# Gates that leave PSUM unscaled: the multiplication by 1/rms moves from the evacuation to the place of use

## The chip, the cores and the metric

The kernel runs on one core of a Trainium2 chip. The metric is the device time of one execution in microseconds (us). Five engines work side by side, each through a queue of its own in program order: TensorE (PE in the profile; its weight loads are listed apart as PEld), VectorE (DVE), ScalarE (ACT), GpSimd (POOL) and SyncE (SP, which here only issues DMAs). They are ordered among each other by semaphores. Matmul results land in PSUM and are copied from there ("evacuated") by VectorE or ScalarE into SBUF.

## The reference

One layer of an encoder on x of 1024 tokens by 1024 features, float32:

```
h    = rms_norm(x, norm_g)
proj = h @ w_in                 # 1536 Hyena columns, 512 gate g_h, q, k, v, 512 gate g_a
y_h  = order-2 Hyena of the 1536 columns (short convolution, then two long FFT convolutions)
y_a  = windowed attention of q, k, v (+-128 tokens, 8 query heads, 2 key heads, a sink)
y    = concat(rms_norm(y_h) * silu(g_h), rms_norm(y_a) * silu(g_a))
x    = x + y @ w_out
```

The first rms_norm has two factors: the weight norm_g per feature, which the kernel puts into its operands, and 1/rms per token. Since a token's 1/rms is the same for all features, it can be applied after the projection: the kernel projects x * norm_g and multiplies the columns of proj, one per token, by the token's 1/rms. The change is about where that is done for g_h and g_a.

## The kernel before, in words

The projection works on tiles of 128 output columns in two halves of 512 tokens, so that a half is a PSUM tile of 128 x 512 with tokens along the free side. Its 8 steps over the features take three matmuls each (L257 to L259: both operands are split into a high and a low part, `w_hi`/`w_lo` and `h`), 24 matmuls for a half. There are two PSUM banks for these halves (`pj`), used in turn. `self.row` holds 1/rms of the 1024 tokens in all 128 partitions.

The order of the projection tiles is a string: Hyena and q/k/v tiles first, then eight gate tiles: four of the Hyena branch (c = 0 to 3), four of attention (c = 4 to 7). `gate_tiles` (L441) computes them; its `evac` calls `scaled` (L268), a VectorE product of the PSUM tile and `self.row` at a raised priority, into one of three SBUF buffers tagged `raw` (named `graw`), and SyncE stores that in the DRAM scratch `gt`. The Hyena tiles use `scaled` too, and are not touched.

Beside the projections runs the other branch, the generator `hyena_branch`: filter spectra, DFTs and inverse DFTs of four quarters of 128 channels, then attention. `weave` mixes the two by fixed costs per step, and a scheduler with priorities then fixes the order of instructions on each engine. The last Hyena quarter ends with VectorE's products `u` (L803) and ScalarE's squares `zsq` (L834), whose sum over quarters is `ztot`. After it attention starts: for every block of 128 tokens q is transposed (aT, bT), scores are computed twice, once for the maxima (`smax`, reduced by VectorE at L945 into `mx`) and once transposed (`st`), VectorE adds a mask to the edges (L983), ScalarE takes the exponential `pf` (L986), TensorE multiplies by the values (`pv`) and VectorE divides (`den`, `ao`).

The gates come back at two places:

- `hyena_output(c)` runs four times between the attention units, behind the sum `ztot` on each engine queue that it uses together with it. It reloads a whole gate row of 128 x 1024 (two buffers, tag `sc`), takes silu as x * (1 + tanh(x/2)) (L1063 on ScalarE, L1064 on VectorE, the factor 1/2 being elsewhere), multiplies with the transposed Hyena output and splits the product into `yh` and `yl`.
- `output_operands(j)` runs once per block of 128 tokens. It reloads 128 x 4 x 128 of the attention gates (tag `ga`, two buffers, so that the load for block j waits until the last reader of block j - 2, the subtraction `al` at L1109, is done), takes silu the same way, multiplies with the transposed attention output and splits it into `ah` and `al`.

The output projection (`po`, L1124 to L1126) takes these operands and the split w_out. The first half of w_out is staged in eight pieces (`output_weights`, while the last gate tiles are projected): POOL issues the load (L1031), ScalarE casts the high part (L1037), VectorE subtracts the low part (L1038); two buffers. The first `po` matmul stands behind the last gate projection. `last_weights` stages the second half in the same way from buffers of the stage pool.

Of the kernel before, what the change touches and what calls it, by code (L numbers as in the profile page):

```python
# [14 lines left out]
ALU = mybir.AluOpType  # L15
# [4 lines left out]
P = 128  # L20
# [21 lines left out]
HP = 200  # L42
# [8 lines left out]
def view(ap, off, dims):  # L51
    return bass.AP(
        tensor=ap.tensor, offset=ap.offset + off, ap=[list(ap.ap[0])] + [list(d) for d in dims]
    )


class Kernel:
# [387 lines left out]
    def gate_tiles(self, cs, sp):  # L445

        nc = self.nc
        ws = [self.next_weights(c) for c in cs]
        pieces = None
        for h in range(2):  # L450
            for c, w in zip(cs, ws):
                if len(cs) > 1 and h == 1 and c == cs[1]:
                    assert self.mixed
                    last = self.last_weights(sp)
                    next(last)

                def evac(h, pt):
                    raw = sp.tile([P, 512], F32, tag="raw", name=self.nm("graw"))
                    self.scaled(raw, pt, h)
                    nc.sync.dma_start(self.gt[:, c, 512 * h : 512 * h + 512], raw)  # L460

                for cost in self.half(w, h, evac):
                    yield cost
                    if pieces:
                        next(pieces, None)
            if len(cs) > 1 and h == 0:
                pieces = self.output_weights()
                next(pieces)
        if len(cs) > 1:
            for _ in chain(pieces, last):  # L470
                pass
        self.gates += len(cs)
# [593 lines left out]
    def hyena_output(self, c, rstd, sp, ps):  # L1066

        nc = self.nc
        V = nc.vector
        g = sp.tile([P, S], F32, tag="sc", name=self.nm("gate"))  # L1070
        nc.sync.dma_start(g, self.gt[:, c])
        self.silu2(g, sp, "t2")
        y = sp.tile([P, 8, P], F32, tag="raw", name=self.nm("y"))
        nc.sync.dma_start(y, self.zd[c])
        V.tensor_tensor(out=y, in0=y, in1=view(rstd, 0, [[1, 8], [0, P]]), op=ALU.mult)
        for h in range(2):
            pt = ps.tile([P, 4, P], F32, tag="t", name=self.nm("yT"))
            for k in range(4):
                nc.tensor.transpose(pt[:, k], y[:, 4 * h + k], self.ident)
            gv = g.rearrange("p (b a) -> p a b", a=8)[:, 4 * h : 4 * h + 4]  # L1080
            V.scalar_tensor_tensor(
                out=gv, in0=pt, scalar=self.gn[:, c : c + 1], in1=gv, op0=ALU.mult, op1=ALU.mult
            )
        nc.scalar.copy(self.yh[:, c], g)
        V.tensor_tensor(out=self.yl[:, c], in0=g, in1=self.yh[:, c].bitcast(F32), op=ALU.subtract)
# [6 lines left out]
    def output_operands(self, j, op, ps):  # L1092

        nc = self.nc
        V = nc.vector
        rows = slice(j * P, (j + 1) * P)
        g = op.tile([P, 4, P], F32, tag="ga", name=self.nm("ga"))
        nc.sync.dma_start(g, self.gt[:, 4:8, rows])
        self.silu2(g, op, "th")
        of = op.tile([P, 512], F32, tag="of", name=self.nm("of"))  # L1100
        nc.sync.dma_start(of, self.od[j])
        pt = ps.tile([P, 4, P], F32, tag="t", name=self.nm("oT"))
        for c in range(4):
            nc.tensor.transpose(pt[:, c], of[:, c * P : (c + 1) * P], self.ident)
        V.tensor_tensor(out=g, in0=pt, in1=g, op=ALU.mult)
        ah = op.tile([P, 4, P], F32R, tag="ah", name=self.nm("ah"), bufs=3)
        al = op.tile([P, 4, P], F32R, tag="al", name=self.nm("al"), bufs=3)
        nc.scalar.copy(ah, g)
        V.tensor_tensor(out=al, in0=g, in1=ah.bitcast(F32), op=ALU.subtract)  # L1109
        return ah, al  # L1110
# [383 lines left out]
```

## Time and profile before

| | us |
|---|---|
| runs | 641.06, 640.04, 639.3 |
| median | 640.04 |
| the profiled execution's own time | 637.56 |
| its span, first to last instruction | 635.8 |
| PE busy / DVE busy / ACT busy in the span | 625.0 / 531.2 / 266.5 |

The profiled execution is a run of its own, a little faster than the three timed ones. Between its span and its time lie 1.76 us at the start and the end. PE's busy time counts a matmul from its start to its modelled end, and matmuls overlap in a pipeline, so it hides short stalls. The granted clock of TensorE is 1.0 throughout. In the timeline `us` is how long an instruction took, and what stands in brackets is how long its engine was idle before it and what released it.

The sixteen gate halves are evacuated between 340.5 and 473.4 us, the first `ztot` is at 408.2, the gates of the Hyena branch are used until 445 (tanh product), those of attention from 491 to 598.

### The profile page before, as it was taken

The numbers are of one execution on the slowest core, as the hardware profiler recorded it, in microseconds if no ns is written. First come the engines' busy times: TensorE is split into PE (matmuls) and PEld (weight loads), VectorE is DVE, ScalarE is ACT, GpSimd is POOL, SyncE is SP. The second block draws the span as 40 slices with busy tenths as digits, with TensorE's granted clock in tenths as the row PEclk, the third lists the DMA queues.
The fourth block names the chain that finished last, engine by engine and source line by source line (L and its number), as shares of the span: only waits on it lengthen the run. The fifth ranks groups of instructions, "written<-read, shape, count | busy, mean of one in ns | idle before, by whom it ended". The sixth has DMA issues, their size and how long they took to land.

```text
span 635.8 us, 10699 instructions
## 1 busy us (share of the span) xinstructions
PE 625.0 (98%) x3994; PEld 553.1 (87%) x3994; DVE 531.2 (84%) x1189; ACT 266.5 (42%) x506; POOL 65.3 (10%) x83
## 2 busy tenths in 40 slices
PE   9999999999999999999999999999998999999997
PEld 7878998989898989899998988888787878888885
DVE  6969699997999997979999899689989888976531
ACT  6766413254432353523443332545465343544210
POOL 0121002021100121211102102100200000000000
PEclk9999999999999999999999999999999999999999
DMA  8966937478574576694548656645645125313321
GB/s 324 281 148 155 296 86 181 126 180 202 147 182 129 148 184 160 138 216 107 134 135 208 184 175 156 188 138 182 207 137 179 56 65 166 105 37 114 100 82 51
DMA packets 47107, 98.37 MB, mean 155 GB/s; under 512 B 6728, under 2 KB 15440, under 8 KB 46800
## 3 DMA queue, kind: packets, MB, share of 16 engines
q1 hardware_dynamic: 32784, 63.79, 30.2%
q0 software_dynamic: 10720, 26.21, 21.8%
q10 hardware_dynamic: 3552, 7.71, 3.5%
q8 instruction: 31, 0.51, 0.3%
q14 instruction: 20, 0.16, 0.1%
HBM read 53.65 MB, written 22.02 MB: 119 GB/s over the span
## 4 chain that ended last, share of the span: by engine, by line
PE 85%; DMA 5%; DVE 4%; issue 3%; ACT 2%; POOL 0%; SPq 0%; POOLq 0%; ACTq 0%; DVEq 0%
PE proj L257 10%; PE proj L258 9%; PE proj L259 9%; PE dft L645 8%; PE pv L1000 5%; PE fw L761 5%; PE po L1124 4%; PE po L1126 4%; PE po L1125 4%; PE inv L802 4%; PE qkv L508 3%; PE qkv L509 3%; PE qkv L510 3%; PE smax L940 1%; PE uT L434 1%
## 5 line engine op out<-in xcount | busy, mean ns | idle before, releaser
L257 PE MATMUL proj<-h,w_hi 128*128 128x512 f32 x304 | 121.5, 400 | 0.0
L259 PE MATMUL proj<-h,w_lo 128*128 128x512 f32 x304 | 119.8, 395 | 0.0
L258 PE MATMUL proj<-h,w_hi 128*128 128x512 f32 x304 | 119.7, 394 | 0.0
L225 POOL DMA_DIRECT2D w_lo<-wraw x48 | 42.2, 896 | 242.3 <-ACT w_lo L224 220.3
L258 PEld LDWEIGHTS proj<-h,w_hi 128*128 128x128 f32 x304 | 57.2, 188 | 11.4 <-issue 0.7
L257 PEld LDWEIGHTS proj<-h,w_hi 128*128 128x128 f32 x304 | 57.2, 188 | 11.3 <-issue 0.7
L259 PEld LDWEIGHTS proj<-h,w_lo 128*128 128x128 f32 x304 | 57.1, 188 | 10.9
L508 PE MATMUL qkv<-w_hi,h 128*128 128x256 f32 x192 | 55.0, 287 | 0.0
L510 PE MATMUL qkv<-w_hi,h 128*128 128x256 f32 x192 | 54.6, 285 | 0.0
L509 PE MATMUL qkv<-w_lo,h 128*128 128x256 f32 x192 | 54.4, 284 | 0.0
L222 ACT CAST w_hi<-wraw 128x512 fp32r<-128x512 f32 x48 | 29.4, 619 | 59.7 <-PE proj L258 36.6
L645 PE MATMUL dft<-eo,d 128*128 128x128 f32 x352 | 45.5, 276 | 1.5 <-DVE eo L629 1.5
L1000 PEld LDWEIGHTS pv<-vv,pf 128*128 128x128 f32 x352 | 44.6, 191 | 2.0 <-DVE ao L1005 0.4
L1000 PE MATMUL pv<-vv,pf 128*128 128x66 f32 x352 | 45.0, 269 | 0.1
L645 PEld LDWEIGHTS dft<-eo,d 128*128 128x128 f32 x352 | 42.5, 192 | 2.0 <-DVE eo L629 1.9
L508 PEld LDWEIGHTS qkv<-w_hi,h 128*128 128x128 f32 x192 | 36.7, 191 | 0.0
L509 PEld LDWEIGHTS qkv<-w_lo,h 128*128 128x128 f32 x192 | 36.7, 191 | 0.0
L510 PEld LDWEIGHTS qkv<-w_hi,h 128*128 128x128 f32 x192 | 36.7, 191 | 0.0
L945 DVE CUSTOM_DVE_ANT_0 mj<-smax,mask 128x384 f32<-128x384 f32 (+1 forms) x64 | 33.2, 519 | 3.7 <-PE smax L940 2.2
L986 ACT ACTIVATE pf<-st 128x768 f32<-128x768 f32 (+1 forms) x32 | 24.3, 758 | 25.5 <-DVE st L983 24.9
L802 PE MATMUL inv<-V,di 128*128 128x128 f32 x256 | 34.8, 275 | 0.0
L1128 DVE TENSOR_TENSOR xr<-po,xr 128x512 f32<-128x512 f32 x22 | 15.1, 688 | 22.0 <-PE po L1126 22.0
(217 smaller groups left out, 1458.2 us busy)
## 6 DMA issues: line engine op xcount, KB each, us to landing
wraw<-in_w_in SPq DMA_DIRECT2D x48, 256.0 KB, 3.7
w_lo<-wraw POOLq DMA_DIRECT2D x48, 256.0 KB, 4.2
hy<-hsc ACTq DMA_DIRECT2D x12, 512.0 KB, 5.9
u<-hy SPq DMA_DIRECT2D x12, 512.0 KB, 6.1
hsc<-hs POOLq DMA_DIRECT2D x9, 511.5 KB, 5.3
hsc<-hraw POOLq DMA_DIRECT2D x9, 511.5 KB, 5.4
x<-in_x_t SPq DMA_DIRECT2D x8, 512.0 KB, 8.9
dec<-in_decay SPq DMA_DIRECT2D x8, 512.0 KB, 4.2
```

Source lines behind the costliest of these rows:

```text
L225: nc.gpsimd.dma_start(l.bitcast(F32), raw, accum_op=ALU.add)
L257: nc.tensor.matmul(pt, hi[:, k], xh, start=k == 0, stop=False)
L258: nc.tensor.matmul(pt, hi[:, k], xl, start=False, stop=False)
L259: i = nc.tensor.matmul(pt, lo[:, k], xh, start=False, stop=k == 7)
L508: nc.tensor.matmul(pt[:, b], hh, hi[:, :, k], start=k == 0, stop=False)
L509: nc.tensor.matmul(pt[:, b], hh, lo[:, :, k], start=False, stop=False)
L510: i = nc.tensor.matmul(pt[:, b], hl, hi[:, :, k], start=False, stop=k == 7)
L645: nc.tensor.matmul(out, m, eo[:, t, e], start=n == 0, stop=n == len(terms) - 1)
L761: nc.tensor.matmul(pt[:, k, c], self.d[:, t + k, c], u[:, t + k], start=True, stop=True)
L802: nc.tensor.matmul(pt[:, k], self.di[:, t + k, c], v[:, t + k, c], start=c == 0, stop=c == 1)
L945: V.tensor_tensor_reduce(out=junk[:, 0:nk], in0=pm[:, 0:nk], in1=mask, op0=ALU.add, op1=ALU.max, scale=1.0, scalar=NEG, accum_out=mx[:, 4 ...
L1000: nc.tensor.matmul(pv[:, h], probs[:, n, cols], self.vv[:, k0 + n, g], start=n == 0, stop=n == nk - 1)
```

## The change

ScalarE copies the gate halves out of PSUM as they are, at the same raised priority, and they are stored so. VectorE multiplies the reloaded gates by `self.row`, in place, before silu: 4 times 128 x 1024 in `hyena_output`, 8 times 128 x 512 in `output_operands`, where the 128 tokens of the block are read four times over.

```diff
@@ gate_tiles, evac @@
                     raw = sp.tile([P, 512], F32, tag="raw", name=self.nm("graw"))
-                    self.scaled(raw, pt, h)
+                    with self.tc.high_priority(HP):
+                        nc.scalar.copy(raw, pt)
                     nc.sync.dma_start(self.gt[:, c, 512 * h : 512 * h + 512], raw)
@@ hyena_output @@
         g = sp.tile([P, S], F32, tag="sc", name=self.nm("gate"))
         nc.sync.dma_start(g, self.gt[:, c])
+        V.tensor_tensor(out=g, in0=g, in1=self.row.rearrange("p h t -> p (h t)"), op=ALU.mult)
         self.silu2(g, sp, "t2")
@@ output_operands @@
         g = op.tile([P, 4, P], F32, tag="ga", name=self.nm("ga"))
         nc.sync.dma_start(g, self.gt[:, 4:8, rows])
+        V.tensor_tensor(out=g, in0=g, in1=view(self.row[:], j * P, [[0, 4], [1, P]]), op=ALU.mult)
         self.silu2(g, op, "th")
```

Lines move by one behind the first edit and by more behind the second and third (the tanh of L1063 is L1064 in the changed kernel, the silu product of L1064 is L1065; the new products are L1073 and L1101). Up to the last Hyena quarter the engines' orders differ only by the moved evacuations. At three places more moves.

On VectorE at the end of the last Hyena quarter, before (`inv` is the inverse transform in PSUM, `kk` belongs to attention's keys, `mx` to the first block's maxima):

```order
L270 TENSOR_TENSOR graw_4083<-proj_3973,row 128x512
L748 SCALAR_TENSOR_TENSOR V_3809<-gm_3821,ml_3811 128x2x128
L803 TENSOR_TENSOR u_3774<-inv_3856,u_3774 128x512
L803 TENSOR_TENSOR u_3774<-inv_3866,u_3774 128x512
L910 TENSOR_TENSOR kk_3986<-qkv_3980,kk_3986 128x2x64
L910 TENSOR_TENSOR kk_4107<-qkv_4101,kk_4107 128x2x64
L1288 TENSOR_REDUCE ztot<-zssq 128x8
L1064 SCALAR_TENSOR_TENSOR gate_4344<-th_4346,gate_4344 128x1024
L270 TENSOR_TENSOR graw_4220<-proj_4086,row 128x512
L945 ISA mj_4022,mx_4005<-smax_4020,mask_3929 128x256
```

and after the change:

```order
L804 TENSOR_TENSOR u_3774<-inv_3856,u_3774 128x512
L804 TENSOR_TENSOR u_3774<-inv_3866,u_3774 128x512
L1291 TENSOR_REDUCE ztot<-zssq 128x8
L1073 TENSOR_TENSOR gate_4344<-gate_4344,row 128x1024
L95 TENSOR_SCALAR rsv_4328<-ztot 128x8
L96 TENSOR_SCALAR rsh_4329<-ztot 128x8
L1073 TENSOR_TENSOR gate_4386<-gate_4386,row 128x1024
L911 TENSOR_TENSOR kk_3986<-qkv_3980,kk_3986 128x2x64
L99 TENSOR_SCALAR rsy_4331<-rsv_4328 128x8
L108 TENSOR_TENSOR rst_4330<-rsy_4331 128x8
L1065 SCALAR_TENSOR_TENSOR gate_4344<-th_4347,gate_4344 128x1024
```

The evacuations of `graw` are gone; two products of 128 x 1024 stand between `ztot` and the first tanh product, and the keys' subtraction comes after them.

On TensorE at attention's first transposes (`aT`), before:

```order
L258 MATMUL proj_4086<-h_90,w_hi 128x512
L259 MATMUL proj_4086<-h_90,w_lo 128x512
L257 MATMUL proj_4243<-h_89,w_hi 128x512
L933 MATMUL aT_4006<-identr,qq_3946 128x128 x4
L933 MATMUL aT_4013<-identr,qq_3946 128x128 x4
L258 MATMUL proj_4243<-h_89,w_hi 128x512
```

and after the change:

```order
L259 MATMUL proj_4086<-h_90,w_lo 128x512
L934 MATMUL aT_4006<-identr,qq_3946 128x128 x4
L257 MATMUL proj_4086<-h_90,w_hi 128x512
L258 MATMUL proj_4086<-h_90,w_hi 128x512
L934 MATMUL aT_4013<-identr,qq_3946 128x128 x4
L941 MATMUL smax_4020<-kt_3940,qa_4011 128x256
```

The transposes stand ten projection matmuls earlier, inside the gate half `proj_4086`.

On VectorE in one of the later attention blocks, after the change (`al_6082` is the last reader of the buffer into which `ga_6400` is loaded):

```order
L1112 TENSOR_TENSOR al_6082<-ga_6067,ah_6081 128x512
L984 TENSOR_TENSOR st_6184<-st_6184,mask_3929 128x256
L1004 TENSOR_TENSOR den_6211<-pv_6204,es_5897 128x2
L1005 RECIPROCAL den_6211<-den_6211 128x2
L1006 TENSOR_TENSOR ao_5998<-pv_6204,den_6211 128x128
L984 TENSOR_TENSOR st_6215<-st_6215,mask_3929 128x256
L1101 TENSOR_TENSOR ga_6400<-ga_6400,row 128x512
L95 TENSOR_SCALAR rsv_6299<-ossq_6297 128x1
```

Before, the first VectorE instruction of this gate was its tanh product at the same place; now the product with `row` stands there, and the tanh product five small instructions later.

## Prediction

> **What bounds the kernel now.** I read the busy table and the chain of waits of the page first, then a table of windows, because the gates live only in the last half of the span.
>
> ```profile
> PE 625.0 (98%) x3994; PEld 553.1 (87%) x3994; DVE 531.2 (84%) x1189; ACT 266.5 (42%) x506; POOL 65.3 (10%) x83
> ...
> PE 85%; DMA 5%; DVE 4%; issue 3%; ACT 2%; POOL 0%; SPq 0%; POOLq 0%; ACTq 0%; DVEq 0%
> ...
> 340.00:400.00 60.00, 60.00 (x341) 52.42 (x340) 55.62 (x93) 18.48 (x37) 7.79 (x9) 1.00 0.66 178
> 400.00:420.00 20.00, 19.88 (x122) 16.19 (x121) 11.81 (x44) 11.28 (x39) 2.86 (x4) 1.00 0.64 188
> 420.00:460.00 40.00, 39.50 (x254) 34.12 (x253) 38.45 (x84) 19.70 (x35) 3.78 (x7) 1.00 0.54 175
> 460.00:480.00 20.00, 19.27 (x125) 16.83 (x125) 16.62 (x59) 12.36 (x21) 1.61 (x3) 1.00 0.47 158
> 480.00:545.00 65.00, 62.53 (x387) 52.11 (x386) 55.97 (x193) 27.51 (x56) 0.00 (x0) 1.00 0.33 104
> 545.00:580.00 35.00, 35.00 (x241) 30.52 (x239) 28.14 (x107) 16.20 (x33) 0.00 (x0) 1.00 0.27 91
> 580.00:606.00 26.00, 25.84 (x157) 22.52 (x157) 13.80 (x54) 9.04 (x18) 0.00 (x0) 1.00 0.25 83
> ```
>
> The columns of a window are its length, then the busy time of PE, PEld, DVE, ACT and POOL with counts, then the granted clock, the DMA share and GB/s. TensorE sets the end: 98% of the span and 85% of the chain, at a full clock. It isn't held up at all between 340 and 400, where the first nine gate halves are evacuated. It loses time from 420 on, most of all in 480 to 545 (2.5 of 65 us), the stretch where VectorE is 56.0/65 = 86% busy. Whom it waits for there is in the waits of TensorE's weight loads from 400 to the end (total, times, longest):
>
> ```profile
> PEld st L977 <- ACT pf L986: 3.4, 7, 1.2
> PEld smax L940 <- DVE mx L945: 2.9, 7, 0.9
> PEld st L978 <- ACT qb L963: 1.9, 5, 0.5
> PEld smax L940 <- ACT qa L935: 1.5, 5, 0.7
> ```
>
> So attention is a ring of three engines. TensorE waits for ScalarE's exponentials and copies (6.8 us) and for VectorE's maxima (2.9 us), and the exponentials in turn wait for VectorE's mask. A change of VectorE's load before 400 should be worth nothing by itself; in the attention stretch it is worth a part of its size.
>
> **The change, part by part.** The prices come from groups (busy us, mean ns of one):
>
> ```profile
> L270 DVE TENSOR_TENSOR graw<-proj,row 128x512 f32<-128x512 f32 x16 | 11.0, 687 | 1.0 <-PE proj L259 0.8
> L721 DVE TENSOR_TENSOR ef<-sm 128x512 f32<-128x512 f32 x8 | 5.5, 687 | 0.0
> L790 DVE TENSOR_TENSOR ism<-X 128x1024 f32<-128x1024 f32 x8 | 9.8, 1223 | 0.2
> L1075 DVE TENSOR_TENSOR y<-y,rsy 128x1024 f32<-128x1024 f32 x4 | 4.9, 1228 | 0.0
> L769 ACT COPY c<-fw 128x512 f32<-128x512 f32 x16 | 9.4, 588 | 36.4 <-PE fw L761 29.8 <-DVE uv L674 5.2 <-DVE t L674 1.5
> ```
>
> *Removed:* 16 VectorE evacuations of 687 ns, 11.0 us. *Added on ScalarE:* 16 copies out of PSUM; L769 is the same copy at the same size, 588 ns, so 9.4 us. *Added on VectorE:* 4 multiplies of 128x1024 (1223 ns by L790, 1228 by L1075, whose operand is repeated as the attention rows' is): 4.9 us, and 8 of 128x512 at 687 ns: 5.5 us. VectorE's whole bill thus falls by only 11.0 - 4.9 - 5.5 = 0.6 us; what counts is where it moves.
>
> The prices take the two memories as equal, since L270 reads PSUM and L721 reads SBUF, and both take 687 ns. [...]
>
> *Up to 400 us.* Nine evacuations leave (the trace has nine L270 gate halves between 340.5 and 399.6), 9 x 0.687 = 6.2 us of VectorE. TensorE is busy 60.00 of 60 us there, so 0 us. The nine copies (5.3 us) fall on a ScalarE busy 18.48 of 60: also 0. What hides both is TensorE's own stream of projections; without it, the copies would cost up to their 5.3 us.
>
> *The head start.* The freed VectorE finishes the last Hyena quarter sooner. By the order, its last inverse transform stands behind 794 projection matmuls before and 775 after; attention's first transposes behind 809 and 799. One projection matmul follows another at 0.226 us (nine starts, first and last):
>
> ```profile
> 341.62 0.39 PE L259 MATMUL proj<-h,w_lo 128*128 128x512 f32 x1
> ...
> 343.43 0.39 PE L258 MATMUL proj<-h,w_hi 128*128 128x512 f32 x1
> ```
>
> (343.43 - 341.62)/8 = 0.226. So 19 matmuls are 4.3 us and 10 are 2.3 us. The lead shrinks on ScalarE, which before waits for VectorE's u and then works without a gap up to attention's first operand at 409.25:
>
> ```profile
> 402.58 1.29 DVE L803 TENSOR_TENSOR u<-inv,u 128x512 f32<-128x512 f32 x2 [1.92 <-PE inv L802]
> 403.31 0.31 ACT L834 ACTIVATE zsq<-u 128x128 f32<-128x128 f32 x1 [8.62 <-DVE u L803]
> ...
> 409.25 1.08 ACT L935 CAST qa<-aT 128x512 fp32r<-128x512 f32 x2
> ...
> L1063 ACT ACT_TABLE_LOAD x1 | 1.3, 1283 | 12.5 <-DMA gate<-gt 12.5
> L1063 ACT ACTIVATE th<-gate 128x1024 f32<-128x1024 f32 x4 | 4.3, 1064 | 1.9 <-DMA gate<-gt 1.9
> ```
>
> After the change the table load (1.28) and the first gate's tanh (1.06) stand inside that busy piece: they used to run at 359 in an idle ScalarE, and now wait for the multiply, which the order has behind the sum of squares `ztot`. One copy (0.59) joins them, while two weight casts (about 1.2) and a copy move behind: net a little over 1 us. TensorE's total work is unchanged, so a lead is worth something only if it is still there when the projections run out at 473. By the order it isn't: the first transposes are 10 matmuls ahead, those of the third attention block level again. The bounds are -2.3 us (all kept) and 0; I take **-0.5**, nearer to 0 because TensorE waits for almost nothing in 400 to 420 (0.12 us).
>
> *Second part, 400 to 475.* Seven evacuations (4.8 us) leave VectorE and four gate multiplies (4.9 us) come: level, **0**. The seven copies are 4.1 us on a ScalarE with 31.7 idle of 75 (11.28 + 19.70 + 12.36 busy): 0 where the wait is not for ScalarE; the third rival holds what it costs if that cover is gone.
>
> *Attention, 475 to 606.* Eight multiplies come and nothing leaves. By the order six stand among the maxima and masks up to about 580, two later, where VectorE is 13.80/26 = 53% busy. Six are 6 x 0.687 = 4.1 us. Bounds: 0, if they all fall into VectorE's 9.0 + 6.9 us of idle time in 480 to 580; 4.1, if each pushes the ring along. TensorE is itself 97.5 of 100 busy there, so much of a VectorE delay is taken up by other ready matmuls: I take a third, **+1.4**. Each multiply also waits for a reload of the gate, priced with the second rival and taken as 0 here.
>
> Sum: -0.5 + 0 + 1.4 = **+0.9 us**. Against the profiled execution, 637.56 us (span 635.8 and 1.76 around it), that is 638.5. This execution lies 2.48 below the median of the runs, 640.04, so on the median I forecast **640.9 us**.
>
> **The rivals.**
>
> *The head start is kept.* If the lead of 2.3 us lives to the end and the multiplies find idle slots: 640.04 - 2.3 = 637.7; 635.7 if the 4.3 us of the inverse transforms are kept. For it: VectorE is 55.62/60 busy before 400 and its u holds ScalarE for 8.6 us. Against it: the order has lost the lead by the third block. [...]
>
> *VectorE waits for the gate's reload.* Before, the tanh on ScalarE takes that wait; now a VectorE instruction does, with the maxima queued behind it and TensorE behind those.
>
> ```profile
> ga<-gt SPq DMA_DIRECT2D x8, 256.0 KB, 2.9
> ...
> ACT th L1063 <- DMA ga<-gt: 9.2, 3, 4.7
> ...
> 538.50 0.38 SPq L1098 DMA_DIRECT2D ga<-gt  x1
> 541.34 0.63 ACT L1063 ACTIVATE th<-ga 128x512 f32<-128x512 f32 x1 [4.66 <-DMA ga<-gt]
> ...
> 586.46 0.16 DVE L1003 TENSOR_TENSOR den<-pv,es 128x2 f32<-128x2 f32 x1 [2.71 <-PE pv L1000]
> ```
>
> A load is issued when the subtraction `al` two blocks earlier frees its buffer, and takes 2.9 us and its 0.4 of issue. Between that `al` and the multiply the order leaves VectorE work of some 4.6, 3.2, 1.5 and 1.75 us in four blocks (the order's instructions at their groups' mean times). The shortfall is 3.3 - 3.2, 3.3 - 1.5 and 3.3 - 1.75, some 3.5 us; the last two fall where VectorE waits for `pv` anyway, as at 586. Hence +0.1 to +3.5 on the sum: 641 to 644.4. It decides once the load lands later than VectorE reaches the multiply.
>
> *The staging of w_out falls behind (slower).* Its buffers go round through a POOL load, a ScalarE cast and a VectorE subtraction, and are wanted by the first output matmul at 473.2.
>
> ```profile
> ACT wo L1037 <- DMA woraw<-in_w_out: 5.5, 3, 2.5
> ...
> 444.26 0.55 POOL L1031 DMA_DIRECT2D woraw<-in_w_out  x1 [24.32 <-DVE wo L1038]
> ...
> 468.72 0.62 ACT L1037 CAST wo<-woraw 128x512 fp32r<-128x512 f32 x1 [2.11 <-DMA woraw<-in_w_out]
> ...
> 470.59 0.69 DVE L1038 TENSOR_TENSOR wo<-woraw,wo 128x512 fp32r<-128x512 f32 x1 [0.44 <-ACT wo L1037]
> ...
> 473.21 0.39 PE L1124 MATMUL po<-wo,yh 128*128 128x512 f32 x1
> ```
>
> After the change all eight subtractions stand behind the two later gate multiplies (2 x 1.22, some 2.4 us more VectorE ahead of them); before, the first stood ahead of the last gate's tanh product. The cover is 473.2 - (470.59 + 0.69) = 1.9 us. A round of load, cast and subtraction late by 2.4 plus the copies in ScalarE's way (two at 0.59) overruns it by 1.7, and qb and pf, queued behind casts that wait for a load, hold the scores for as long as the 2.11 seen: about +2 to the sum, 643. From 1.9 us of delay it decides.
>
> *The change doesn't do what it says* is ruled out: the order shows 16 copies on ScalarE and 12 multiplies on VectorE, and no L270 on gates.
>
> **How the numbers follow.** A measurement of this kernel tells about 0.3%, 1.9 us, from no change: 638.1 to 642.0 counts as the same. Chances: the forecast (a small loss, own range 639 to 642.5) 0.42, of which 0.33 the same, 0.07 slower, 0.02 faster. Head start kept 0.26: 0.21 faster, 0.05 the same. Reload 0.12: 0.11 slower, 0.01 the same. Staging 0.20: 0.17 slower, 0.03 the same. Together faster 0.23, same 0.42, slower 0.35. The range is 636.5 to 645.0: below, more than the whole lead at the transposes but not all of that at the inverse transforms; above, just past the end of the dearer rivals.
>
> **What would show it.** The window 340 to 400 with VectorE near 49.4 and TensorE still at 60; the copies near 588 ns and the multiplies near 687 and 1223; the first L935 copy at about 407 to 408 and the first `po` matmul within a microsecond of 473.2; TensorE's idle time in 480 to 545 up from 2.5 to about 4. A first `po` at 471 speaks for the head start, one at 475 with longer woraw waits for the staging, and rows of VectorE's idle time ended by `DMA ga<-gt` of over 1 us for the reload. A time below 636.5 or above 645 would mean that a mechanism is missing here.

## The result and the profile after

The changed kernel takes **645.57 us** (median of 6 runs, 643.04 to 649.73) against 639.95 us of the kernel before (6 runs, 639.3 to 641.8): a ratio of 1.0083, with a 95% interval of 1.0054 to 1.0112. It is slower by about 5.6 us. I had forecast 640.9 with 636.5 to 645.0, "no measurable change" the likeliest: the sign of the lean was right, the size was not, and the time lies above the range. Ratios and intervals, here and below, leave out executions in a slow state (one of e3, 661.83 us, one of e14, 873.85, and one of the kernel before, 1578.42); they are still in the medians.

The profiled execution took 645.56 us, with a span of 643.6 us against 635.8 before. First the busy table, the chain's shares and the groups of the added instructions:

```profile
PE 628.0 (98%) x3994; PEld 556.6 (86%) x3994; DVE 532.1 (83%) x1185; ACT 275.9 (43%) x522; POOL 65.1 (10%) x83
...
PE 84%; DVE 8%; DMA 5%; ACT 2%; issue 2%; ACTq 0%; DVEq 0%
...
L460 ACT COPY graw<-proj 128x512 f32<-128x512 f32 x16 | 9.3, 584 | 10.0 <-PE proj L259 6.6 <-issue 3.4
L1101 DVE TENSOR_TENSOR ga<-ga,row 128x512 f32<-128x512 f32 x8 | 5.5, 683 | 1.6 <-DMA ga<-gt 1.6
L1073 DVE TENSOR_TENSOR gate<-gate,row 128x1024 f32<-128x1024 f32 x4 | 4.9, 1214 | 0.2 <-DMA gate<-gt 0.2
```

The prices are as forecast (584 for 588 ns, 683 for 687, 1214 for 1223). VectorE's share of the chain has doubled, from 4 to 8%. Where the time went is in the same windows as before:

```profile
340.00:400.00 60.00, 57.19 (x320) 49.78 (x319) 50.61 (x84) 20.06 (x43) 7.20 (x9) 0.97 0.61 162
400.00:420.00 20.00, 18.78 (x106) 15.02 (x104) 11.55 (x39) 12.85 (x36) 2.29 (x3) 1.00 0.50 141
420.00:460.00 40.00, 39.55 (x257) 33.87 (x257) 33.54 (x69) 20.66 (x39) 2.71 (x5) 1.00 0.52 168
460.00:480.00 20.00, 20.00 (x131) 17.70 (x129) 17.67 (x65) 12.01 (x22) 3.77 (x7) 1.00 0.53 175
480.00:545.00 65.00, 60.68 (x372) 51.19 (x371) 56.47 (x176) 30.79 (x60) 0.00 (x0) 0.97 0.34 110
```

TensorE was busy for the whole of 340 to 400 before; now it stands for 2.8 us there, in the very stretch where I had put every effect at 0, and the granted clock is below 1 in two windows in which it was 1.00. The waits of TensorE from 340 to 640 name the places:

```profile
PE inv L803 <- DVE V L735: 2.8, 1, 2.8
PE smax L941 <- DVE mx L946: 1.9, 2, 1.2
PE aT L934 <- ACT kt L919: 1.6, 2, 1.2
```

The first is the last Hyena quarter's inverse transform. The timelines follow it back. VectorE, TensorE and ScalarE after the change (in brackets the idle time and its releaser):

```profile
395.56 2.04 PE L803 MATMUL inv<-V,di 128*128 128x128 f32 x8 [2.81 <-DVE V L735]
...
382.10 0.69 DVE L904 TENSOR_TENSOR qq<-qkv,qq 128x512 fp32r<-128x512 f32 x1 [2.92 <-ACT qq L903]
...
378.05 0.21 ACT L905 CAST qq<-mask 128x8 fp32r<-128x8 f32 x1 [6.67 <-DMA sink<-in_attn_sink]
378.16 0.62 ACT L903 CAST qq<-qkv 128x512 fp32r<-128x512 f32 x1
378.68 0.20 ACT L905 CAST qq<-mask 128x8 fp32r<-128x8 f32 x1
380.74 0.31 ACT L852 ACTIVATE gqk<-gqk 128x128 f32<-128x128 f32 x1 [1.86 <-DMA gqk<-in_qk_g]
...
381.45 0.61 ACT L903 CAST qq<-qkv 128x512 fp32r<-128x512 f32 x1
```

and the same instructions before:

```profile
397.14 1.06 PE L802 MATMUL inv<-V,di 128*128 128x128 f32 x8
...
381.50 0.69 DVE L903 TENSOR_TENSOR qq<-qkv,qq 128x512 fp32r<-128x512 f32 x1
...
378.67 0.31 ACT L851 ACTIVATE gqk<-gqk 128x128 f32<-128x128 f32 x1
```

Without the evacuations VectorE reaches attention's `qq` early, at 379.2, and there finds itself behind ScalarE, which waits for two small tables (sink, then gqk). The wait is not only VectorE's being early, for gqk also lands later than before:

```profile
370.02 0.64 ACT L224 ACTIVATE w_lo<-wraw 128x512 fp32r<-128x512 f32 x1
371.02 0.86 POOL L225 DMA_DIRECT2D w_lo<-wraw  x1 [16.23 <-PE fw L762]
372.07 0.44 ACTq L851 DMA_DIRECT2D gqk<-in_qk_g  x1
```

Its load lands 8.7 us behind its issue (372.07 to 380.74), where before it took at most 5.9 (issued at 372.76, no wait at 378.67). More had moved than the evacuations: the first gate's tanh and two pairs of weight casts had stood on ScalarE from 359 to 364, and GpSimd's transfers of `w_lo` behind these casts at 363 and 364; now such a transfer starts at 371.02, just ahead of the tables' loads. In all traces of kernels with the gqk scaling at its old place it is the same: with the Hyena copies (the change, e2, e3, e5, e13) that transfer is at 370.7 to 371.7 and gqk takes 8.0 to 8.7 us, without them (before, e4, e6, e7, e10) the transfer is at 364.6 or earlier and gqk takes at most 6.5. That the one causes the other was not tested.

With ScalarE's second `qq` ready at 380.0 as before, VectorE would have waited some 0.8 us (an estimate). As it is, it stands for 2.92 us, and what the evacuations had freed is mostly gone: `V` is ready about 1.5 us earlier than before (L734/L735 start at 394.99 after 396.46). But the order of TensorE had been made for the whole relief: the inverse transforms stand 19 projection matmuls earlier, 19 x 0.226 = 4.3 us of work. TensorE arrives 4.3 - 1.5 = 2.8 us too soon, and the projections that could have filled the time stand behind in its queue: none starts in the 2.81 us before 395.56. Behind this pause, and behind three shorter ones at 490 to 493, the clock falls (in the rows of windows the granted clock is the third number from the end):

```profile
392.00:394.00 2.00, 0.74 (x4) 0.28 (x2) 2.00 (x4) 0.00 (x0) 0.00 (x0) 1.00 0.90 214
394.00:396.00 2.00, 0.44 (x2) 0.47 (x3) 2.00 (x6) 0.91 (x3) 0.00 (x0) 0.89 0.32 123
396.00:398.00 2.00, 2.00 (x10) 1.90 (x10) 2.00 (x7) 0.42 (x1) 0.86 (x1) 0.50 0.17 31
398.00:400.00 2.00, 2.00 (x9) 1.59 (x8) 0.43 (x2) 1.12 (x2) 0.28 (x1) 0.76 0.58 100
...
490.00:492.00 2.00, 0.77 (x3) 0.45 (x3) 2.00 (x6) 0.00 (x0) 0.00 (x0) 1.00 0.77 191
492.00:494.00 2.00, 1.36 (x5) 0.83 (x5) 1.97 (x7) 1.06 (x2) 0.00 (x0) 1.00 0.84 230
494.00:496.00 2.00, 2.00 (x8) 1.62 (x8) 1.96 (x8) 0.00 (x0) 0.00 (x0) 0.64 1.02 340
496.00:498.00 2.00, 2.00 (x7) 1.62 (x6) 0.79 (x3) 0.00 (x0) 0.00 (x0) 0.51 0.41 129
...
489.90 0.67 PE L941 MATMUL smax<-kt,qa 128*128 128x384 f32 x2 [0.43 <-ACT qa L936]
491.80 0.44 PE L941 MATMUL smax<-kt,qa 128*128 128x384 f32 x1 [1.23 <-DVE mx L946]
492.88 0.44 PE L941 MATMUL smax<-kt,qa 128*128 128x384 f32 x1 [0.64 <-DVE mx L946]
```

The missing clock, summed, is (0.11 + 0.50 + 0.24) x 2 = 1.7 us at the first place and (0.36 + 0.49) x 2 = 1.7 us at the second, where a wait for ScalarE's `qa` and two for VectorE's maxima come one after another. The first output matmul is at 478.03 in place of 473.21, 4.8 us late, of which the stall and the clock behind it make 2.8 + 1.7 = 4.5. Another 2.4 us are lost between there and 506 (the 133rd `pv` matmul stands at 505.94 in place of 498.75), and the second fall of the clock is 1.7 of them.

### The profile page after: what moved, and what is told of

It is laid out like the page before. It is cut to its first block, busy times and chain, and to the rows that moved or that the text cites. A ratio compares the mean times of both kernels' runs of the same rounds, so it can differ in the third digit from the quotient of the medians.

```text
span 643.6 us, 10697 instructions
## 1 busy us (share of the span) xinstructions
PE 628.0 (98%) x3994; PEld 556.6 (86%) x3994; DVE 532.1 (83%) x1185; ACT 275.9 (43%) x522; POOL 65.1 (10%) x83
## 4 chain that ended last, share of the span: by engine, by line
PE 84%; DVE 8%; DMA 5%; ACT 2%; issue 2%; ACTq 0%; DVEq 0%
PE proj L257 9%; PE proj L259 9%; PE proj L258 9%; PE dft L646 8%; PE pv L1001 5%; PE fw L762 5%; PE po L1127 4%; PE po L1128 4%; PE po L1129 4%; PE inv L803 4%; PE qkv L509 3%; PE qkv L511 3%; PE qkv L510 3%; PE smax L941 2%; PE uT L434 1%
## 5 line engine op out<-in xcount | busy, mean ns | idle before, releaser
L803 PEld LDWEIGHTS inv<-V,di 128*128 128x128 f32 x256 | 33.3, 195 | 4.1 <-issue 3.2
```

The lines of the kernel that those rows point to most:

```text
L803: nc.tensor.matmul(pt[:, k], self.di[:, t + k, c], v[:, t + k, c], start=c == 0, stop=c == 1)
```

## The experiments

Theory A, from the trace: the loss starts with the wait for gqk and the early place of the inverse transforms. Theory B, from the prediction: it is what the multiplications cost where they are used. Ratios are to the kernel before, run on the same chip.

| run | what is changed against the kernel before | median us | ratio | 95% interval |
|---|---|---|---|---|
| change | all gates | 645.57 | 1.0083 | 1.0054 to 1.0112 |
| e1 | all gates, gqk scaled later | 642.46 | 1.0054 | 1.0027 to 1.0082 |
| e2 | all copies, no multiplication | 643.53 | 1.0063 | 1.0035 to 1.0091 |
| e3 | Hyena gates | 656.33 | 1.024 | 1.0178 to 1.0301 |
| e4 | attention gates | 636.88 | 0.9958 | 0.9930 to 0.9986 |
| e5 | Hyena copies, no multiplication | 642.48 | 1.0052 | 1.0025 to 1.0079 |
| e6 | Hyena multiplications added, evacuation as before | 641.48 | 1.0031 | 1.0002 to 1.0059 |
| e7 | attention copies, no multiplication | 634.35 | 0.9918 | 0.9893 to 0.9943 |
| e8 | e4, gqk scaled later | 637.43 | 0.9959 | 0.9936 to 0.9982 |
| e9 | e1 without the Hyena multiplications | 641.57 | 1.0040 | 1.0018 to 1.0062 |
| e10 | e4, multiplications on GpSimd | 635.76 | 0.9938 | 0.9918 to 0.9958 |
| e11 | gqk scaled later, nothing else | 637.38 | 0.9964 | 0.9948 to 0.9979 |
| e12 | e1 without the attention multiplications | 639.10 | 1.0000 | 0.9982 to 1.0018 |
| e13 | all gates, inverse transforms put back | 639.88 | 0.9992 | 0.9965 to 1.0019 |
| e14 | e5, gqk scaled later | 639.31 | 0.9985 | 0.9954 to 1.0017 |
| e15 | e10, gqk scaled later | 635.05 | 0.9915 | 0.9884 to 0.9946 |

### e1: take away VectorE's wait

```diff
 attention_setup
-        nc.scalar.mul(self.gqk[:, 0], self.gqk[:, 0], 0.125)
 attention_max, behind the qa copies
+        if j == 0:
+            with self.tc.issue_after(acopy.ins):
+                nc.scalar.mul(self.gqk[:, 0], self.gqk[:, 0], 0.125)
```

> The changed kernel, with one ScalarE instruction moved: the scaling of the small table gqk, which waits for a DMA of its own, stands behind the first block's qa copies instead of ahead of the keys' and queries' copies. What is computed is the same. Theory A (the change's loss begins where VectorE waits 2.9 us for ScalarE's qq behind gqk, so that V is late, TensorE stands at the inverse transforms that the order has put 19 projection matmuls earlier, and the granted clock falls): VectorE's idle time before L903/L904 falls from 2.9 to below 1 us, the stall at inv from 2.8 to at most 1 us, no window below a clock of 0.95 between 390 and 400, and the time falls by 3 to 4.5 us to 641 to 642.5. Theory B (the loss is the multiplications at the place of use and the waits they bring): no change, 645 to 646. Theory C (the earlier place of the inverse transforms alone makes the stall, whatever VectorE waits for): the stall stays over 2 us, 644 to 646.

The stall is gone: TensorE's and VectorE's timelines of this run have no wait at these places,

```profile
393.16 1.13 PE L803 MATMUL inv<-V,di 128*128 128x128 f32 x8
...
379.70 0.69 DVE L903 TENSOR_TENSOR qq<-qkv,qq 128x512 fp32r<-128x512 f32 x1
```

the clock is 1.00 throughout 390 to 404, and the first output matmul is at 474.46 (after the change 478.03). So the chain gqk, qq, V, inv is shown. The time fell by 3.1 us to 642.46, at the edge of the 641 to 642.5 of theory A; by the ratios alone (1.0054 and 1.0083, overlapping intervals) the fall would not be certain. And 2.6 us over the kernel before remain. In the profile TensorE waits 1.9 us for the maxima between 480 and 500 (1.2 in the kernel before), and the granted clock is below 1 twice, from 489.7 and from 537.5 (0.50 for 3.4 us each); whether that is all was not taken apart.

### e2: the copies without the multiplications

```diff
 hyena_output
-        V.tensor_tensor(out=g, in0=g, in1=self.row.rearrange("p h t -> p (h t)"), op=ALU.mult)
 output_operands
-        V.tensor_tensor(out=g, in0=g, in1=view(self.row[:], j * P, [[0, 4], [1, P]]), op=ALU.mult)
```

> The changed kernel without its 12 multiplications (the gates are used without the factor 1/rms; that product is left out of the computation). Theory A: the stall at the inverse transforms and the low clock behind it stay, about 4.8 us at the last projection as in the changed kernel, and only the loss after it (about 3 us) goes: 642 to 644. Theory B: nothing of the loss is left and VectorE has 11 us less to do: 637 to 640.

With 10.4 us less VectorE work than the changed kernel it takes 643.53: theory B (637 to 640) falls, and the time lies in A's range (642 to 644). The stall is there, 2.75 us long. The clock behind it is not lower in this profile, though, so that part of A failed:

```profile
392.00:394.00 2.00, 0.38 (x2) 0.00 (x0) 2.00 (x5) 0.00 (x0) 0.00 (x0) 1.00 0.87 234
394.00:396.00 2.00, 0.87 (x8) 0.90 (x9) 2.00 (x7) 1.34 (x3) 0.23 (x1) 1.00 0.19 72
396.00:398.00 2.00, 2.00 (x12) 1.65 (x11) 2.00 (x6) 1.12 (x2) 0.63 (x1) 1.00 0.45 79
```

### e3 and e4: one half of the gates at a time

```diff
 gate_tiles, evac (e3: c < 4; e4: c >= 4), and only the matching multiplication
-                    with self.tc.high_priority(HP):
-                        nc.scalar.copy(raw, pt)
+                    if c < 4:
+                        with self.tc.high_priority(HP):
+                            nc.scalar.copy(raw, pt)
+                    else:
+                        self.scaled(raw, pt, h)
```

> Only the four Hyena gates are changed (8 ScalarE copies, 4 multiplications of 128x1024); the attention gates are scaled by VectorE when they leave PSUM, as before. The order has the last inverse transforms at the early place (775 projection matmuls). Theory A: stall and low clock there as in the changed kernel, 643 to 645. Theory B: only half the multiplications, and the later ones are the dearer, 641 to 642.

> Only the four attention gates are changed (8 ScalarE copies, 8 multiplications of 128x512); the Hyena gates are scaled by VectorE as before. The order has the last inverse transforms at the old place (794). Theory A: no stall over 1 us there, clock 1.00 between 390 and 400; what is left is the attention stage, +1 to +3 us: 641 to 643. Theory B: most of the loss, 643 to 645.

Both expectations were missed, on opposite sides. The attention half makes the kernel *faster*, 636.88, although six of its eight multiplications fall into the busiest stretch; the inverse transforms stand at the old place and the clock is 1.00 up to 606. The Hyena half alone costs 15 us, by four runs that spread from 651.51 to 661.83. It has the stall at the transforms, and it is the one run in which the staging of w_out breaks down as my third rival had it. ScalarE's, VectorE's and GpSimd's waits of e3 between 396 and 500:

```profile
ACT wo L1041 <- DMA woraw<-in_w_out: 12.5, 4, 8.8
...
DVE tab L877 <- DMA tab<-in_rope: 3.7, 1, 3.7
...
POOL woraw L1053 <- DVE yl L1090: 9.5, 2, 8.9
```

GpSimd's queue has all four loads of the second half of w_out ahead of the third piece of the first half; the last of them waits 8.9 us for VectorE's `yl` of the last gate, and the cast on ScalarE behind it 8.8 us. In the full change this wait is 2.7 us, so this is not what made its 5.6 us.

### e5 to e7: copies and multiplications apart

e5 is e3 without its multiplication, e7 is e4 without its own; e6 keeps the evacuation of the kernel before and adds the four Hyena multiplications.

> Only the four Hyena gates leave PSUM by ScalarE, and their multiplication by 1/rms is left out altogether; the attention gates as before. The order has the last inverse transforms at the early place (775) and the POOL loads of w_out nearly as before. Theory A (two separate losses: the early inverse transforms come with the Hyena copies, and the Hyena multiplications push the staging of w_out back): stall at inv of 2 to 3 us, no wait of ScalarE for woraw above 3 us, 641 to 643.5. Rival D (the Hyena multiplications alone make the whole loss): 638 to 640.

> The kernel before with the four multiplications of the Hyena gates added (VectorE still scales when it evacuates, so these gates are scaled twice). Inverse transforms at the old place (794); in the POOL queue all four loads of the second half of w_out stand ahead of the third piece of the first half. Theory A: no stall at inv; ScalarE waits over 5 us for woraw, the first po matmul is 3 us or more later than in the kernel before, granted clock below 1 behind that; 643 to 650. Rival E (what the multiplications cost is only VectorE's 4.9 us more work): 641 to 644, no long wait for woraw.

> Only the four attention gates leave PSUM by ScalarE, and their multiplication is left out. Against the run with these gates fully changed (636.88) this gives the price of the eight multiplications among attention's maxima and masks. The prediction's term: they cost 1.4 us (bounds 0 and 4.1), so 635.5 (632.8 to 636.9). Rival F (they are free, VectorE has room for them): 636.5 to 637.5.

The four parts, as shares of 640 us: Hyena copies +0.52% (+3.3 us), Hyena multiplications +0.31% (+2.0), attention copies -0.82% (-5.2), attention multiplications 0.9958 - 0.9918 = +0.40% (+2.6). e5 has the stall (2.87 us) and falls into theory A's range.

e6 has no stall at the transforms, as expected, but ScalarE's waits for woraw are 6.4 us in total (5.5 before), and its first output matmul is earlier than before, not later: its 641.48 misses theory A's range and lies in rival E's (641 to 644), beyond the noise only just. Neither picture is shown, though. In the profile TensorE stands 0.5 us at 480.3 for VectorE's `wo` (the staging) and 1.2 us at 482.2 for VectorE's `ao`, and behind that the granted clock is 0.50 from 482.7 to 493.0, which is worth 5.1 us (the mean clock of this execution is 0.992 over 639.2 us): more than this kernel loses in all. The low clock is what theory A had behind the staging; how much of it is the staging's, and how much VectorE's other work, these runs don't tell.

e7's 634.35 lies below the 635.5 expected, inside the bounds, and rival F missed. The parts sum to +2.7 us; measured together they make +5.3 (1.0083). For the Hyena half, +5.3 by the parts stand against +15 (e3). They don't add. Each changes the order of all queues; which of these changes makes the difference was not separated. Nor was what the attention copies' 5.2 us come from followed in the traces.

### e8 and e11: gqk later where there is no such stall

> Only the four attention gates are changed, as in the fourth run, and gqk is scaled later, as in the first. Theory A: VectorE reaches qq only after ScalarE has it in this order (it still evacuates eight gate halves), so the move is worth nothing here: 636 to 637.5. Rival: gqk holds something else too, 635 or less.

> The kernel before with gqk scaled later, nothing else changed. Theory A: VectorE gets to qq after ScalarE has it, so no stall is taken away: within 0.3% of the kernel before, 638.5 to 641.5. Rival: the move is good in itself, and the first run's 3 us say nothing about the change: 636 to 638.

With the attention gates alone it is worth nothing (0.9959 for 0.9958), as expected. On the kernel before it gives 1.8 us (637.38 for 639.20), which theory A excluded. So the 3.1 us of e1 can't all be put down to the stall: another order of the queues further on is worth as much elsewhere.

### e9 and e12: what remains in e1

> The first run's kernel (all gates changed, gqk scaled later) with the four Hyena multiplications left out. What is left against the kernel before are the copies and the eight attention multiplications, without the stall at the inverse transforms. Theory A (what remains of the loss, 642.46 against 640, is the Hyena multiplications: they stand ahead of the table load and the keys' copies, and among the staging of w_out): 637 to 639.5. Rival G (the remaining loss is the early place of the inverse transforms itself, or chance of the clock): 641 to 643.

> The first run's kernel with the eight attention multiplications left out, the four Hyena ones kept. If these eight cost the same here as alone (2.5 us), 640. If the remaining loss is mainly the Hyena multiplications, it is still above the kernel of the ninth run: 639 to 641.5; if the attention multiplications make it, 637 to 638.5.

Theory A missed e9: without the Hyena multiplications 641.57 remain, so they are not what is left in e1. e12 is level with the kernel before: in this surrounding the attention multiplications cost 642.46 - 639.10 = 3.4 us. With the copies of the Hyena gates and no stall, e9 is still 0.8% above e4, which leaves the early place of attention's start or the copies themselves. (e8 is the nearer comparison, with gqk late too: 0.9959, the same.) TensorE's waits of e9 between 440 and 500 are all for VectorE:

```profile
PE smax L943 <- DVE mx L948: 2.1, 2, 1.2
PE bT L963 <- DVE rsh L96: 1.7, 1, 1.7
PE yT L1082 <- DVE gate L1084: 0.6, 1, 0.6
```

### e13: put the inverse transforms back

```diff
 long_conv, last convolution of the last quarter only
-            with self.tc.high_priority(-HB):
+            with self.tc.high_priority((-HB - 30) if self.lastc else -HB):
```

> The full change, with the last two inverse transforms at a priority lower by 30, so that the order has them between 783 and 791 projection matmuls, spread, in place of 767 and 775 (the kernel before: 786 and 794); gqk is scaled where it was. Theory H (the early place is what costs: TensorE comes to the transforms before V is there): stall at inv below 0.5 us, VectorE's 2.9 us wait for qq is still there and costs nothing, 640 to 642.5. Rival I (the copies of the Hyena gates cost wherever the transforms stand): 644 to 646.

This decides it. All gates are copied and multiplied as in the change, and VectorE's wait is still there,

```profile
382.51 0.69 DVE L906 TENSOR_TENSOR qq<-qkv,qq 128x512 fp32r<-128x512 f32 x1 [2.87 <-ACT qq L905]
...
PE inv L803 <- DVE V L749: 0.4, 1, 0.4
```

but TensorE, which now does projections meanwhile, waits for `V` only 0.4 us. The time is 639.88, ratio 0.9992: the 5.6 us are gone, and the interval (0.9965 to 1.0019) lies clear of that of the change. It went a little further than theory H expected (640 to 642.5). One caution: the lower priority also moved things behind, by a few matmuls (the first transposes stand behind 813 projection matmuls in place of 807), and the 1.2 us that the change loses at `aT` is absent here too. And e11 shows that another order alone can be worth 1.8 us. So what is shown is that the early place, with what moved with it, costs the 5.6 us to within an amount of that size, not that the one stall does.

### e14: the Hyena copies without the wait

> Only the four Hyena gates leave PSUM by ScalarE, their multiplication left out (as in the fifth run, 642.48), and gqk is scaled later. Theory H: the stall at inv falls below 1 us and with it 3 us or more of the time: 637 to 639.5, level with the kernel before with gqk late (637.38). Rival J (the earlier start of attention makes new waits for VectorE behind it, as large as the stall): 640.5 to 643.

639.31, inside the noise of the kernel before and 3 us below e5, near the upper end of theory H's range. Alone, the Hyena copies cost through the stall; without it they are worth nothing either: 0.9985 against e11's 0.9964, with overlapping intervals. Beside the changed attention gates that doesn't hold: there e9 (1.0040) lies 0.8% above e8 (0.9959), which differs from it by the Hyena copies alone, and has no stall at the transforms. What makes this rest stays open.

### e10 and e15: what the parts point to

```diff
 output_operands, attention gates only (e4), e10:
-        V.tensor_tensor(out=g, in0=g, in1=view(self.row[:], j * P, [[0, 4], [1, P]]), op=ALU.mult)
+        nc.gpsimd.tensor_tensor(out=g, in0=g, in1=view(self.row[:], j * P, [[0, 4], [1, P]]), op=ALU.mult)
```

> Only the four attention gates are changed, and their eight multiplications run on GpSimd, which issues nothing after 480 us, in place of VectorE. If the 2.5 us between the fourth and the seventh run are VectorE's time among the maxima, this gets most of it back: 634 to 636. If they are the wait for the gate's reload ahead of tanh, or GpSimd is slow enough to be waited for (over 3 us an instruction), 637 to 640.

> Only the attention gates changed, their multiplications on GpSimd (tenth run, 635.76), and gqk scaled later (eleventh run, -1.8 us on the kernel before). If the two add up: 633.5 to 635; if gqk is worth nothing here, as with the attention gates on VectorE (eighth run against the fourth): 635 to 636.5.

GpSimd, idle from 480 on, takes 1307 ns for what VectorE does in 683 (the change), and ScalarE's tanh waits for it, 19.1 us in all, on an engine that is not the bound:

```profile
L1103 POOL TENSOR_TENSOR ga<-ga,row 128x512 f32<-128x512 f32 x8 | 10.5, 1307 | 120.0 <-DMA ga<-gt 62.8 <-DMA of<-od 21.4 <-DVE rst L105 19.7
L1067 ACT ACTIVATE th<-ga 128x512 f32<-128x512 f32 x8 | 5.0, 631 | 19.1 <-POOL ga L1103 19.1
```

About half of the multiplications' 2.6 us seems to come back (0.9938, between 0.9958 and 0.9918; the intervals overlap). With gqk later as well, e15 takes 635.05, ratio 0.9915 (0.9884 to 0.9946): faster than both kernels, by 4.6 us than the one before and by some 10 than the change. Whether gqk adds to e10 is not told by these runs, since the intervals overlap.

## Why the prediction was wrong

- **The head start** is the step that failed, by its sign. "The bounds are -2.3 us (all kept) and 0" took an earlier place in TensorE's queue for an earlier time, or at worst for nothing. It is an obligation: the transforms stood first in TensorE's queue without being ready, and held up all behind for 2.81 us. `V` came 1.5 us earlier, the queue wanted it 4.3 us earlier, and the difference was a stall of 2.8 us and, in this execution, 1.7 us of clock. Some 2 of these 2.8 us are gqk's later landing (the estimate above), which no term had either. With the transforms put back (e13) the full change measures 639.88, near the 640.9 forecast; that nearness is partly luck, since two other terms below are off in opposite directions. I had even read the two numbers (794 and 775) in the order, and not asked whether VectorE could keep them; the row of its `qq` behind ScalarE, and ScalarE's behind three small DMAs (a wait of 5.87 us before, covered), were in the trace. (In the traces the first transposes stand behind 817 and 807 projection matmuls by the count that gives 794 and 775, not 809 and 799; the ten between them, on which the sum rests, are right.)
- **"What hides both is TensorE's own stream of projections"**: VectorE's busy time there fell to 50.61 (49.4 forecast), and the Hyena copies alone were indeed worth about nothing once the stall was away (e14 against e11). But the stream hid a late VectorE only where the order let projections go first: TensorE waited 0.4 us for `V` in e13, 2.8 in the change.
- **400 to 475, "level, 0"** netted VectorE's time over different places. Apart, the attention copies are worth -5.2 us and the Hyena multiplications cost +2.0. The sum is nearer to -3 than to 0, as far as parts that don't add can say; for the attention half alone the kernel gets faster, which none of my cases had.
- **The attention multiplications**, +1.4 with bounds 0 and 4.1: measured +2.6 (e7 to e4) and +3.4 (e1 to e12). Inside the bounds, mis-sized by a factor of two.
- **The reload**: VectorE waited 1.6 us in all for `ga<-gt`, at most 1.0 at once; how much of it reached TensorE was not followed. It is too little to make 5.6 us.
- **The staging rival** gave 643, for a reason that isn't this kernel's: the wait of ScalarE for woraw fell from 5.5 to 2.7 us. Its mechanism exists, and e3 shows it at 8.8 us.
- **The prices** and the count of moved instructions were right to 1%. Taking the two memories as equal was right as well: a product of 128x512 took 683 ns from SBUF (L1101 after the change) and 687 from PSUM (L270 before).
- **The clock** was missing from the sum. In the change the windows show 0.50 for 3.41 us at two places, 1.7 us each. The pauses ahead of it were 2.8 us at the first place, and three of 0.4 to 1.2 us at 490 to 493 at the second; behind 2.75 us in e2's profile it stayed at 1.00.

## What to carry to other kernels

When a list scheduler fixes in-order queues, an engine that is relieved on paper moves its consumers forward in the other queues; before counting the lead, look in the trace whether the producer can really deliver at the new place, because here nothing filled the gap behind an instruction that already stood at the head (2.81 us in the change, 2.75 in e2). Look along the relieved engine for the next wait that the old work had covered (here small DMAs), and let a consumer stand a few instructions late rather than early. And take such a change apart by its halves: here one half was worth -3 us and the other cost more than that.

## What was not expected of the hardware

A pause of TensorE cost about 1.7 us more than its length where the granted clock fell behind it. The values of 0.51 to 0.89 in the tables above are windows of 2 us that a fall covers in part. Windows cut to fit show 0.50 for 3.41 us (the change: 395.56 to 398.97 and 494.55 to 497.96) and 1.00 on both sides, so that each fall cost 3.41 x 0.5 = 1.7 us. In e6 one lasts three times as long, 10.24 us.

It didn't always fall: the stalls of 2.81 us (the change) and 2.75 us (e2) at the same instruction ended with and without it. How busy TensorE was around them doesn't tell them apart either: from 392 to 396 it is busy for 0.74 + 0.44 = 1.18 of 4 us in the change and for 0.38 + 0.87 = 1.25 in e2. In the 3.41 us ahead of the fall it is busy for 18% in the change (392.14 to 395.56) and for some 35% in e3. Two falls of one profile start 98.99 us apart in the change and, by windows of 2 and 4 us, some 47.8 in e1 and 71.7 in e3 (estimates), which is 29.0, 14.0 and 21.0 times the 3.41 us that one lasts. What decides whether a pause ends in a fall was not shown: no run moved a pause on purpose.

Between executions of one kernel the clock makes much of the spread: the mean clock of the change's six runs is 0.987 to 0.997 at spans of 647.7 to 641.0 us, and span times clock is 637.9 to 640.4, under half as wide. The profile of the kernel before had a clock of 1.000, where most of its other runs lie between 0.993 and 0.997, which is probably part of why it lay 2.5 us below the median.
